# An encoder block on one core: its input projection by seven block products in planned order, and one branch's output product moved into the attention

## The chip, the core and the metric

The kernel runs on one core of a Trainium2 chip. The core has a matrix engine (TensorE, PE in the profile; PEld is its weight load), a vector engine (VectorE, DVE), a scalar engine (ScalarE, ACT), GpSimd (POOL) and SyncE (SP), which here does nothing but issue DMAs. Each engine works through its own queue in order and waits on semaphores. Sixteen DMA engines move data between the device memory (DRAM) and the on-chip memory of 128 partitions; matmuls write into PSUM, a small memory of eight banks of 128 x 512 float32.

The metric is the device time of one execution in microseconds (us). Less is better.

## What is computed

The input x has 2048 tokens of width 1024, in float32. `proj = rms_norm(x) @ w_in` has 4608 columns, which are split into u and v (512 each), q, k and v of an attention (512 each), and two gates of 1024 each.

```python
z_a = gelu(proj[..., :1024])
y_a = gmlp_spatial_gating(z_a[..., :512], z_a[..., 512:], ...)   # layer norm of v, mixing in chunks of 128 tokens, times u
y_b = neighbourhood_attention_2d(q, k, v, ...)                   # q, k normed per head; 8 heads, windows of 8 x 16 on a 32 x 64 grid
gates = sigmoid(gate_pre + b_gate)
merged = gates[..., :1024] * (y_a @ w_o_a) + gates[..., 1024:] * (y_b @ w_o_b)
x = x + merged @ w_out
x = x + square(relu(rms_norm(x) @ w_ff1)) @ w_ff2                # inner width 4096
```

## The kernel before, in words

**Products.** A float32 operand is split into a high part (a cast on ScalarE to fp32r) and a low part (the remainder, on VectorE), and a product is made of three matmuls: high by high, high by low, low by high. One matmul takes a 128 x 128 tile of weights and 512 columns. A product of 128 x 512 with an inner width of 1024 is thus 24 matmuls (`gemm`, L335).

**Order of the work.** The first part, up to the end of the attention, is written as a list: `run` (L1345) calls for each half h of 1024 tokens `gmlp` (L522: u, then v with its layer norm and the spatial mixing `mix`, L577), `att_v` (L640), `qk` (L595) for q and for k, then `gate_units` (L652). Weights are loaded (`load_wk`, L327) and split just ahead; x times the norm's gain is split once for each half (`parts`, L452) and kept on chip in 16 tiles `hT`. The framework's own scheduling sets the order on the engines. `later` and `flush` (L343, L347) put transposes and mixing some products after the work that they wait for. Results go to DRAM: `ya` (first branch, split), `qs`, `ks`, `vs`, and `gt` (gates, 256 KB a tile). `bias_tables` (L396) makes the attention's bias tables by DMAs of GpSimd.

**The attention** (`attention`, L802) has 16 units (4 pairs of heads by 4 row blocks) of 4 steps each. A step i does the scores of step i (`att_scores`: matmuls, a minimum and bias on VectorE, exp on ScalarE, the normalising on VectorE), the transposes of step i-1 (`att_turn`) and the values of step i-2 (`att_values`). Keys come through GpSimd's queue, the rest (`qn`, `vw`, `bias`) through SP's, one unit ahead. Between the steps, `fill` takes the gate tiles of the second half, 24 matmuls each: of 32, up to the 28th is spread over the 64 steps, and 4 follow after.

**The second part** has another discipline: `Plan` (L81). Steps are the pieces of PE work in a fixed order, with a cost in us; chains are stages (loads, casts, remainders, sums) with a cost, an engine and a lead before the step that needs them. `Plan.run` gives each stage the latest step by which it must be issued, issues earlier what fits an engine's modelled clock and the 51 buffers (`NBUF`) of 4 KB per partition, and so writes the engines' order out. `rest` (L1320) puts into one plan, for each half: `merge` (L1001: both branch products, 12 matmuls each, times their gates, added and split), `out_proj` (L1067), `up` (L1198) and `down` (L1280).

**Seven block products.** `up` and `down` cut each operand into 2 x 2 blocks and form seven products of sums of blocks instead of eight (`seven`, L957). The sums of weights are made by four GpSimd operations for each 256 columns (`w_seven`, L893; L909 to L916), those of activations likewise, stored in DRAM as seven parts (`hf`, `af`) and loaded and split again by `x_seven` (L925), in 28 buffers for one operand. One unit of seven products of 4 blocks is 84 matmuls.

Of the kernel before, what the change touches and what calls it, by code (L numbers as in the profile page):

```python
# [12 lines left out]
F32 = mybir.dt.float32  # L13
# [60 lines left out]


# [5 lines left out]
class Plan:  # L81
# [24 lines left out]
    def run(self):  # L106
# [5 lines left out]
        release = [[] for _ in range(n)]  # L112
        for c in self.chains:
            due = at[c.first] if c.first is not None else at[min(n, c.start + 1)] + c.due
            low = (c.start + 1) if c.start is not None else 0
            c.low = min(low, n - 1)
            c.latest = []
            for st in c.stages:
                i = n - 1
                while i > c.low and at[i] > due - st.lead + 1e-9:  # L120
                    i -= 1
                c.latest.append(max(i, c.low))
            for k in range(len(c.latest) - 2, -1, -1):
                c.latest[k] = min(c.latest[k], c.latest[k + 1])
        for _ in range(3):
            for c in self.chains:
                for a, k in c.after:
                    for j in range(k):
                        a.latest[j] = min(a.latest[j], c.latest[0])
# [17 lines left out]
        active, nxt = [], 0  # L147

        def issue(c, i, t):
            k = c.done  # L150
            st = c.stages[k]
            b = max(c.ready, clock.get(st.eng, 0.0), t)
            clock[st.eng] = b + st.cost
            c.ready = b + st.cost + st.wait
# [17 lines left out]
        for i, s in enumerate(self.steps):  # L172
# [5 lines left out]
            for c in active:  # L178
# [3 lines left out]
                if k > c.done:  # L182
                    force(c, k, i, t0)
                    if c.first is not None and c.first <= i:
                        now = max(now, c.ready)
# [5 lines left out]
            for c in active:  # L191
                if c.low > i:
                    continue
                while c.done < len(c.stages):
# [5 lines left out]
                    b = max(r, clock.get(st.eng, 0.0), now)  # L200
# [4 lines left out]
                    c.ready = r  # L205
# [22 lines left out]
class Block:  # L228


    def __init__(self, ctx, tc, a):
        self.ctx, self.tc, self.nc, self.a = ctx, tc, tc.nc, a
        self.waiting = []
        self.second, self.free = False, []
# [16 lines left out]

        self.x1 = d("x1", [2, 8, P, 1024])
# [4 lines left out]
    def first_part(self):  # L257
# [6 lines left out]
        self.part = part  # L264

    def second_part(self):

        self.part.close()
        self.second = True
        self.more = self.ctx.enter_context(self.tc.tile_pool(name="more", bufs=1, reuse_waits="tile"))  # L270
        self.free = list(range(NBUF))

# [5 lines left out]
    def give(self, *ts):  # L278
        self.free += [t for t in ts if t is not None]

    def new(self, shape, dt, name, tag="act"):

        return self.take(shape, dt, name) if self.second else (None, self.slot(shape, dt, name, tag))
# [37 lines left out]
    def split_w(self, raws, name, pool=False):  # L321

        per = raws[0].shape[1]
# [1095 lines left out]
```

## Time and profile before

| | |
|---|---|
| median of 3 runs | 2731.29 us (2729.28 to 2735.18) |
| profiled execution, its own time | 2733.02 us |
| its span, first to last instruction | 2730.6 us |
| mean granted clock of PE in it | 0.982 of full |
| busy: PE, VectorE, ScalarE, GpSimd | 2620.1, 1667.3, 975.4, 869.0 us |
| moved by DMA | 474.11 MB |

The span of the trace runs: input projection to about 666 us, attention to about 1008, the last gate tiles to about 1031, merge and output product to about 1438, then the feed-forward part. Busy time of PE is modelled, since matmuls are pipelined; the distance between the starts of two matmuls tells what one costs. In the rows, `fg<-hT,wg_hi` means that tile fg is written from hT and wg_hi; "x1024" counts instructions; the number after the comma is the mean duration in ns; behind the bar stands the idle time before them and what ended it. In tables of windows, the numbers after the window and its length are busy us of PE, PEld, DVE, ACT and POOL with instruction counts in brackets, then the granted clock of PE, the DMA engines' busy share and GB/s.

### The profile page before, as it was taken

The page shows a single profiled execution, that of the slowest core. Times are in us where ns is not written, and L with a number is a line of the kernel's source. Part 1 is how long each engine was busy: PE and PEld are TensorE (multiplying, and loading weights), DVE is VectorE, ACT ScalarE, POOL GpSimd, SP SyncE. Part 2 cuts the span into 40 slices and gives each one's busy share as a digit, 9 for nine tenths or more (in the row PEclk, how much of TensorE's full clock was granted, in tenths as well). Part 3 has the DMA queues.
Part 4 walks back from the last instruction along what each step waited for, and adds up shares of the span by engine and source line. Part 5 has one row for each costly group of instructions (what it writes and reads, how often), then busy time and mean ns, then how long its engine had stood idle before and what let it go on. Part 6 is the DMA issues. An engine that isn't in the chain of part 4 may idle for free. (4 is left out here: it accounts for less than half of the span.)

```text
span 2730.6 us, 33775 instructions
## 1 busy us (share of the span) xinstructions
PE 2620.1 (96%) x12228; PEld 2133.0 (78%) x12228; DVE 1667.3 (61%) x2574; ACT 975.4 (36%) x1567; POOL 869.0 (32%) x640
## 2 busy tenths in 40 slices
PE   8999999999999997998998999899998999979999
PEld 7888888887777775886876888678886888868887
DVE  6545225546766652543547666788877566588886
ACT  6333225322433321234243434434334343443331
POOL 0005500002121200020035767633433676734341
PEclk9999999999999998999999999999999999989999
DMA  6358842456888838268283444644445544464442
GB/s 193 112 132 199 235 141 89 118 126 150 241 246 231 233 111 308 78 229 326 77 302 129 134 163 148 256 164 158 149 138 195 170 137 160 164 252 141 165 141 104
DMA packets 324630, 474.11 MB, mean 174 GB/s; under 512 B 29485, under 2 KB 215252, under 8 KB 324464
## 3 DMA queue, kind: packets, MB, share of 16 engines
q1 hardware_dynamic: 310176, 444.13, 50.7%
q0 software_dynamic: 13248, 27.82, 4.0%
q8 instruction: 97, 1.59, 0.2%
q14 instruction: 69, 0.57, 0.1%
q10 hardware_dynamic: 1040, 0.00, 0.0%
HBM read 310.78 MB, written 161.04 MB: 173 GB/s over the span
## 5 line engine op out<-in xcount | busy, mean ns | idle before, releaser
L977 PE MATMUL z<-x_t,t_hi 128*128 128x512 f32 x1024 | 321.8, 396 | 39.9 <-DVE x L1304 30.7
L340 PE MATMUL fg<-hT,wg_hi 128*128 128x512 f32 x1024 | 331.4, 398 | 0.0
L870 DVE TENSOR_TENSOR r_lo<-w_r,r_hi 128x1024 fp32r<-128x1024 f32 (+3 forms) x140 | 212.3, 1516 | 81.6 <-ACT r_hi L866 81.6
L977 PEld LDWEIGHTS z<-x_t,t_hi 128*128 128x128 f32 x1024 | 194.4, 191 | 85.7 <-ACT a_B L1226 13.9
L340 PEld LDWEIGHTS fg<-hT,wg_hi 128*128 128x128 f32 x1024 | 191.4, 189 | 44.5 <-issue 8.4
L909 POOL TENSOR_TENSOR w_s<-w_r 128x512 f32<-128x512 f32 (+3 forms) x70 | 98.9, 1412 | 361.1 <-PE y L977 265.8
L977 PE MATMUL z<-x_t,t_lo 128*128 128x512 f32 x512 | 202.2, 395 | 5.7 <-DVE t_lo L870 5.7
L340 PE MATMUL fg<-hT,wg_lo 128*128 128x512 f32 x512 | 202.2, 395 | 0.0
L977 PE MATMUL x<-x_r,t_hl 128*128 128x512 f32 x768 | 192.0, 398 | 6.8 <-DVE t_hl L870 6.8
L977 PEld LDWEIGHTS x<-x_r,t_hl 128*128 128x128 f32 x768 | 147.8, 193 | 39.5 <-DVE t_hl L870 7.6
L866 ACT CAST r_hi<-w_r 128x1024 fp32r<-128x1024 f32 (+3 forms) x140 | 135.9, 972 | 76.3 <-PE z L977 50.2
L340 PE MATMUL fg<-mg,w_out_hi 128*128 128x512 f32 x512 | 160.5, 394 | 2.1 <-DVE mg L1059 2.1
L977 PE MATMUL z<-x_t,r_hi 128*128 128x512 f32 x512 | 159.1, 392 | 2.7 <-DVE x L1304 2.6
L1304 DVE TENSOR_TENSOR x<-z,x 128x512 f32<-128x512 f32 x152 | 104.2, 686 | 90.3 <-PE z L977 90.2
L977 PE MATMUL z<-x_r,r_hi 128*128 128x512 f32 x512 | 159.3, 393 | 0.0
L977 PE MATMUL y<-x_r,r_hi 128*128 128x512 f32 x512 | 158.5, 391 | 0.0
L977 PE MATMUL x<-x_r,r_hi 128*128 128x512 f32 x512 | 157.6, 389 | 0.0
L665 DVE TENSOR_TENSOR g<-fg,rs_row 128x512 f32<-128x512 f32 x64 | 44.1, 691 | 172.1 <-PE fg L340 171.5
L1130 POOL TENSOR_TENSOR h_t<-h,h 128x512 f32<-128x512 f32 x8 | 10.6, 1321 | 390.4 <-ACT h L1119 390.4
L949 DVE TENSOR_TENSOR x_r<-x_r,x_r 128x1024 fp32r<-128x1024 f32 x80 | 131.8, 1660 | 1.5 <-ACT x_r L945 1.5
L870 DVE TENSOR_TENSOR t_lo<-w_s,t_hi 128x1024 fp32r<-128x1024 f32 (+3 forms) x70 | 126.6, 1808 | 3.0 <-ACT t_hi L866 3.0
L687 POOL DMA_DIRECT2D kst<-ks x32 | 24.1, 753 | 322.6 <-DVE y L584 186.2
(219 smaller groups left out, 6060.5 us busy)
## 6 DMA issues: line engine op xcount, KB each, us to landing
w_r<-in_w_ff_dram SPq DMA_DIRECT2D x116, 512.0 KB, 4.4
x_r<-af SPq DMA_DIRECT2D x64, 512.0 KB, 4.5
x<-in_xT_dram SPq DMA_DIRECT2D x32, 512.0 KB, 9.5
wg<-in_w_in_dram SPq DMA_DIRECT2D x32, 512.0 KB, 7.6
gt<-g SPq DMA_DIRECT2D x64, 256.0 KB, 3.0
qn<-qs SPq DMA_DIRECT2D x64, 256.0 KB, 4.9
g<-gt SPq DMA_DIRECT2D x32, 512.0 KB, 12.4
x<-x SPq DMA_DIRECT2D x32, 512.0 KB, 9.0
```

The lines of the kernel that those rows point to most:

```text
L340: self.nc.tensor.matmul(out, w[p], x[q], start=(i == 0 and j == 0), stop=(i == n - 1 and j == 2))
L665: nc.vector.tensor_tensor(g, pt, rs[b][1], ALU.mult)
L687: nc.gpsimd.dma_start(k.rearrange("p r c -> p (r c)"), self.ks[:, :, hd, pair, r0 * GW : (r0 + n) * GW].rearrange("l d t -> (l d) t"),)
L866: nc.scalar.copy(e[name + "_"][1][0], e[name][1])
L870: nc.vector.tensor_tensor(lo, e[name][1], hi.bitcast(F32), ALU.subtract)
L909: nc.gpsimd.tensor_tensor(s23[:, :, 1], r1[:, :, 0], r1[:, :, 1], ALU.subtract)
L949: nc.vector.tensor_tensor(lo, lo.bitcast(F32), hi.bitcast(F32), ALU.subtract)
L977: nc.tensor.matmul(out, a[u], b[v], start=(p in (1, 5, 2) and k == 0 and j == 0), stop=(k == n - 1 and j == 2), skip_group_check=p in (6, ...
L1130: nc.gpsimd.tensor_tensor(t[0][1][:, 1], v[:, 1], u[:, 1], ALU.subtract)
L1304: nc.vector.tensor_tensor(v, bank, v, ALU.add)
```

## The change

- The first part becomes a plan of its own (`first_steps`), with the same 51 buffers. `first_u` makes u of the first half by direct products in quarter steps from x in pieces of 256 KB, and forms the sums of blocks of x on GpSimd. Gates of both halves and u of the second half are units of seven products (`feat`). v with the attention's v (`values`), and q with k (`queries`), are seven products with tokens as rows (`seven_tok`): one slice has 4 x 128 columns of each of the seven parts of x, and the block sums of the weights stay on chip for 8 slices (28 buffers).
- The operands of these go through DRAM: sums of x in `xf`, sums of weights in `wf`, u in `ut`. `x_slice` loads a slice in four DMAs with runs of 512 bytes.
- Gates get their sigmoid before they are stored, in both halves.
- `bias_tables` becomes a chain of GpSimd stages in the plan.
- The attention stays a list. Its filler is no longer gate tiles: `branch_units` makes the 32 tiles of the first branch's output product (12 matmuls each), times the gate, into `ma`. 26 of them are spread (2 ahead), 6 follow.
- `merge` has the second branch's product only; `ma` is added on GpSimd.
- The planner orders what follows what by chains (`hf_done`, `af_done`) instead of given steps, and its costs for loads and GpSimd are lower.

The diff, cut to its core:

```diff
+        self.ut = d("ut", [AW, S])
+        self.ma = d("ma", [D, S])
+        self.xf = d("xf", [2, P, 7, 4, 512])
+        self.wf = d("wf", [2, P, 7, 4, 512])
...
-    DMA, CAST, SUB, ADD = 3.0, 1.06, 1.25, 0.7
-    PSUM_DVE, PSUM_ACT, POOL, MM = 0.7, 0.6, 1.9, 0.2267
+    DMA = 1.6
+    POOL, MM = 1.5, 0.2267
...
+    def feat(self, h, xs, c0, row, act, dst, leads=(26, 15, 10)):
+        w = self.w_seven(self.a["w_in"][0], [0, 2, 4, 6], [1, 3, 5, 7], c0, leads)
...
+        ids = self.seven(w, xs, {1: copy(0, 0, True), 5: copy(1, 1, True), 6: copy(0, 1, False), 3: add(0, 1), 7: add(1, 1),
+                                 2: add(0, 0), 4: (lambda bank: fin(1, 0, bank), 0, {"DVE": 0.7, "ACT": 0.7}, 0)})
...
+    def x_slice(self, h, t):
...
+                src = self.xf[h][:, p0:p1, :, t * P : (t + 1) * P] if n == 2 else self.xf[h][:, p0, :, t * P : (t + 1) * P]
+                nc.sync.dma_start(lo.bitcast(F32), src)
...
+    def seven_tok(self, ws, x, evac, mid):
...
+                for k in range(4):
+                    a = [v[:, k] if xi is None else v[:, xi, k] for v in x[0][xn][1]]
+                    b = [v if wi is None else v[:, wi] for v in ws[k][0][wn][1]]
+                    for j, (u, v) in enumerate(((0, 0), (0, 1), (1, 0))):
+                        nc.tensor.matmul(out, a[u], b[v], start=(p in (1, 5, 2) and k == 0 and j == 0),
+                                         stop=(k == 3 and j == 2), skip_group_check=p in (6, 3, 7, 4))
...
+    def first_steps(self):
+        plan = self.plan = Plan(NBUF)
+        xs = self.first_u()
...
+        for c in range(8):
+            if c < 2:
+                self.first_w(0, c, len(plan.steps) + 5)
+            elif c < 6:
+                self.rows_out(1, c - 2, len(plan.steps) + 5, norm)
...
+            gates(0, xs, c)
...
+        xs = [self.x_seven(self.xf[1][:, :, c], (self.xf_done[1, c],)) for c in range(4)]
...
+            self.feat(1, xs, C_U + c * 256, lambda b: self.rows["in", 1, b], act,
...
+            gates(1, xs, c)
+        for p, f in ((0, self.values), (1, self.queries)):
+            ws = [self.x_seven(self.wf[p][:, :, c], (self.wf_done[p, c],)) for c in range(4)]
+            for h in range(2):
+                for t in range(4):
+                    f(h, t, ws)
...
+        self.bias_tables(mark, end)
+        plan.run()
...
+    def branch_units(self):
+        ys = []
+        for b in range(4):
+            ys.append([])
+            for k in range(4):
+                y = self.slot([2, 512], F32R, "y")
+                nc.sync.dma_start(y.bitcast(F32), self.ya[:, :, k, b * 512 : b * 512 + 512])
+                ys[b].append(y)
+        load = lambda c: self.load_wk(a["w_o_a"][0], c * 256, 256, 4, "woa", True) if c < 4 else None
...
+            g, at = gs.pop(0)
+            pt = self.feat_gemm(w, mm, ys[b], 4)
+            nc.vector.tensor_tensor(g, pt, g, ALU.mult)
+            nc.sync.dma_start(self.ma[at], g)
+            yield
...
-            for name, src in (("ya", self.ya), ("yb", self.yb)):
...
+                        for i, (src, j) in enumerate(((self.ma, m), (self.gt, m + 8))):
+                            nc.sync.dma_start(e["g"][1][:, i], src[j * P : (j + 1) * P, tok : tok + 512])
...
+                    def add(e=e):
+                        g = e["g"][1]
+                        nc.gpsimd.tensor_tensor(g[:, 0], g[:, 0], g[:, 1], ALU.add)
...
+        with self.plan_part("one"), self.tc.manual_schedule():
+            self.first_steps()
+        with self.list_part():
+            self.units, self.bias = {}, {}
+            self.load_unit(0)
+            units = self.branch_units()
+            next(units)
+            next(units)
+            done = 2
...
+                while done < 26 and done < 2 + (step + 1) * 24 / 64:
+                    next(units)
+                    done += 1
...
+        with self.plan_part("two"), self.tc.manual_schedule():
             self.rest()
```

In `first_u`, x comes in pieces of 128 x 512 and each product of u is four steps of six matmuls:

```diff
+                    nc.sync.dma_start(e[raw][1][:, b], a["xT"][k * P : (k + 1) * P, b * 512 : b * 512 + 512])
...
+                for q in range(4):
+                    ks = range(2 * q, 2 * q + 2)
+                    need = [w[g // 2][q // 2][1]] + [A[b, k] for k in ks]
+                    i = plan.step(6 * self.MM, lambda ks=ks: prod(ks), need)
```

In `queries`, each of the four results of a slice (q and k of two token tiles) goes through these stages before its transposes:

```diff
+                ch = plan.chain([Stage("ACT", 0.65, square, 1, 0, 8, 0.3), Stage("DVE", 0.9, factor, 0, 1, 6, 0.6), Stage("DVE", 1.4, scale, 0, 0, 3, 0.2)], start=i)
+                self.todo.append((delay, lambda: turn(ch)))
```

## Rows read from the trace of the kernel before

**Rows 1.** The page, busy us of PE, share of the span, instructions.

```profile
PE 2620.1 (96%) x12228; PEld 2133.0 (78%) x12228; DVE 1667.3 (61%) x2574; ACT 975.4 (36%) x1567; POOL 869.0 (32%) x640
```

**Rows 2.** The chain that ended last: start us, us, what; a feed-forward piece.

```profile
1478.98 2.72 PE z L977 x12
```

**Rows 3.** Windows of 100 us: the first, and one within `up`.

```profile
0.00:100.00 100.00, 91.58 (x421) 74.86 (x422) 61.16 (x106) 50.38 (x80) 0.70 (x6) 1.00 0.49 153
...
1500.00:1600.00 100.00, 100.00 (x443) 82.84 (x442) 61.21 (x60) 40.39 (x58) 66.75 (x41) 1.00 0.44 150
```

**Rows 4.** Groups of instructions by line, PE, high part: gates, one projection, u.

```profile
L340 PE MATMUL fg<-hT,wg_hi 128*128 128x512 f32 x1024 | 331.4, 398 | 0.0
...
L340 PE MATMUL tg<-wk_hi,hT 128*128 128x512 f32 x256 | 82.9, 395 | 0.0
...
L340 PE MATMUL fg<-hT,wu_hi 128*128 128x512 f32 x256 | 82.0, 399 | 8.3 <-ACT hT L455 7.8 <-DVE z L534 0.3
```

**Rows 5.** Groups by line, POOL: one of four sums of blocks in `out_proj`.

```profile
L1131 POOL TENSOR_TENSOR h<-h 128x512 f32<-128x512 f32 x8 | 11.2, 1398 | 0.6
```

**Rows 6.** Windows of 100 us: three changes of operands in the feed-forward part.

```profile
1700.00:1800.00 100.00, 87.20 (x367) 69.98 (x367) 74.13 (x77) 42.33 (x60) 55.94 (x40) 0.95 0.67 242
2000.00:2100.00 100.00, 89.05 (x378) 72.17 (x376) 76.86 (x85) 37.72 (x49) 32.12 (x24) 0.97 0.57 195
2400.00:2500.00 100.00, 86.08 (x350) 68.80 (x351) 81.67 (x87) 40.78 (x51) 37.38 (x21) 0.91 0.55 193
```

**Rows 7.** The chain that ended last, at the first of these.

```profile
1751.38 9.05 DMA x_r<-af
1762.11 7.84 DMA af<-a_A
```

**Rows 8.** Timeline of PE at the end of the queries: start, us, what, idle before.

```profile
665.68 1.08 PE L623 MATMUL qT<-ident,qn 128*128 128x128 f32 x4 [5.95 <-DVE qn L611]
...
673.67 0.60 PE L623 MATMUL qT<-ident,qn 128*128 128x128 f32 x4
674.03 0.71 PE L340 MATMUL fg<-hT,wg_hi 128*128 128x512 f32 x2
```

**Rows 9.** Groups by line, DVE: operations of queries and keys, and one remainder of weights.

```profile
L605 DVE TENSOR_REDUCE qms<-sq 128x8 f32<-128x512 f32 x32 | 21.9, 684 | 62.6 <-ACT sq L603 62.6
L611 DVE TENSOR_TENSOR qn<-tg,qrs 128x512 f32<-128x512 f32 x32 | 22.1, 691 | 1.9 <-DVE qrs L609 1.0
L626 DVE SCALAR_TENSOR_TENSOR qo<-qT,qg,qo 128x512 fp32r<-128x512 f32 x16 | 11.9, 744 | 1.5 <-ACT qo L625 1.5
L364 DVE TENSOR_SCALAR rsq_t<-rsq_t 128x8 f32<-128x8 f32 (+1 forms) x44 | 10.7, 242 | 1.4
L609 DVE TENSOR_SCALAR qrs<-qrs,rs_col 128x8 f32<-128x8 f32 x32 | 10.2, 318 | 1.1
L308 DVE TENSOR_TENSOR wq_lo<-wq,wq_hi 128x1024 fp32r<-128x1024 f32 x8 | 9.8, 1226 | 55.7 <-ACT wq_hi L307 54.9
```

**Rows 10.** Groups by line, POOL: DMAs that write the bias tables.

```profile
L424 POOL DMA_DIRECT2D tb<-tbi x72 | 43.0, 600 | 31.5 <-DMA tb<-tbi 26.7 <-DMA tb<-tbt 3.5 <-issue 0.9
```

**Rows 11.** The attention as one window: all instructions; those of the gates (L340) alone.

```profile
666.00:1008.00 342.00, 336.42 (x2178) 259.38 (x2178) 223.43 (x750) 127.81 (x395) 66.04 (x55) 0.99 0.79 218
...
666.00:1008.00 342.00, 183.55 (x672) 122.80 (x672) 0.99 0.79 218
```

**Rows 12.** DMA issues between 680 and 1000 us: count, KB each, us to landing.

```profile
wg<-in_w_in_dram SPq DMA_DIRECT2D x12, 512.0 KB, 7.6
```

**Rows 13.** Windows of 10 us: early attention, start of the merge, end of `out_proj`.

```profile
690.00:700.00 10.00, 10.00 (x69) 7.14 (x69) 7.83 (x30) 3.85 (x14) 1.06 (x2) 1.00 1.06 257
1040.00:1050.00 10.00, 5.80 (x12) 3.63 (x12) 1.23 (x1) 1.04 (x1) 0.00 (x0) 0.55 1.02 364
1400.00:1410.00 10.00, 10.00 (x45) 8.26 (x44) 3.72 (x5) 2.31 (x3) 9.25 (x7) 1.00 1.03 416
```

**Rows 14.** Timeline of PE at the start of the merge.

```profile
1043.28 1.22 PE L340 MATMUL fg<-y,w_o_a_hi 128*128 128x512 f32 x2 [12.58 <-ACT w_o_a_hi L866]
```

More of the change, by code (lines that the diff above doesn't have):

```diff
@@ L73, in __init__, with begin @@
         self.ends = []
+    def begin(self):
+        k = self.done
+        return 0.0 if k and self.stages[k].eng == self.stages[k - 1].eng else self.ready
 class Step:
@@ L147, in run @@
         active, nxt = [], 0
+        needs = [[] for _ in range(n)]
+        for c in self.chains:
+            if c.first is not None and c.last is not None:
+                needs[c.first].append(c)
         def issue(c, i, t):
@@ L183, in run @@
                     force(c, k, i, t0)
-                    if c.first is not None and c.first <= i:
-                        now = max(now, c.ready)
+            now = max([now] + [c.ready for c in needs[i]])
             late = now - t0
@@ L278, in give @@
     def give(self, *ts):
-        self.free += [t for t in ts if t is not None]
-    def new(self, shape, dt, name, tag="act"):
-        return self.take(shape, dt, name) if self.second else (None, self.slot(shape, dt, name, tag))
+        self.free += ts
     def slot(self, shape, dt=F32, name="slot", tag="act"):
@@ new lines, in stores, with out, f @@
+    def stores(self, e, names, dst, give):
+        def out(name, part, kept):
+            def f():
+                p0, p1 = self.X_PART[part]
+                self.nc.sync.dma_start(dst[:, p0:p1] if p1 - p0 == 2 else dst[:, p0], e[name][1])
+                if kept:
+                    self.give(e[name][0])
+            return f
+        return [Stage("SP", self.DMA if p != "t4" else 0.5 * self.DMA, out(n, p, g), 0, int(g), 3 - 0.5 * i, 2.0)
+                for i, (n, p, g) in enumerate(zip(names, ("r1", "r2", "t23", "t4"), give))]
@@ new lines, in first_w, with load @@
+    def first_w(self, pair, c, due):
+        cols = ((C_V, C_AV), (C_Q, C_K))[pair]
+        e = {}
+        st = []
+        for i, raw in ((0, "w1"), (1, "w2")):
+            def load(e=e, raw=raw, k=2 * c + i):
+                e[raw] = self.take([2, 512], F32, raw)
+                for j in range(2):
+                    self.nc.sync.dma_start(e[raw][1][:, j], self.a["w_in"][0][k * P : (k + 1) * P, cols[j] : cols[j] + 512])
+            st.append(Stage("SP", 3.0, load, 1, 0, 26, 3.0))
+        st += self.sums(e, "w1", "w2", "t23", "t4", "S")
+        st += self.stores(e, ("w1", "w2", "t23", "t4"), self.wf[pair][:, :, c], (True,) * 4)
+        ch = self.plan.chain(st)
+        ch.first = due
+        self.wf_done[pair, c] = (ch, len(st))
@@ L1185, in turn_evac @@
             nc.scalar.copy(row, own["pt"])
-            self.rows[h, b] = row
+            self.rows[key, h, b] = row
+            self.cols[key, h, b] = own["col"]
             if b == 1:
```

1061 lines of the change are left out of this document (651 added, 410 removed).

## The prediction

> **What bounds the kernel now.** I read the busy table first: TensorE (PE) is busy in 96% of the span [rows 1]. A busy PE need not be PE at its peak, so the chain that ended last came next: in a stage without waits it consists of pieces of twelve matmuls that take 2.72 us, 0.2267 us for each [rows 2]. The table of 100 us stretches shows PE without a gap in such a stage, and a gap of 8.4 us in the first stretch [rows 3]. So the kernel is bound by the number of its matmuls, plus some 110 us of gaps. Where a change takes matmuls out, the question is what new gaps it opens, and whether another engine or the DMA is next in line.
>
> **Matmuls removed.** The groups of PE by line give the counts [rows 4]: gates 1024 with the high part of the weights (the low part has half as many, as everywhere), so 1536; the four projections of which wk is one, 384 each; wu 384. That is 3456 matmuls. In the new kernel the first half's u stays direct (192). All else goes through seven block products instead of eight: 3264 x 7/8 = 2856. So 408 matmuls go, 408 x 0.2267 = **-92.5 us**, all of it on PE, which sets the end. The two branch products keep their number (768); half of them move into the attention. Work in transposes, spatial mixing and norms stays.
>
> **The start.** x arrives in 256 KB pieces and u goes in quarter steps. The gap was 8.4 us [rows 3]; the first product still waits for one weight tile, one piece of x and their casts. Between -2 and +10; I take **+2**.
>
> **Block sums of x.** They can start only when a block's scaled casts and squares are done, and the gates need all of them. They are 16 GpSimd operations like the one of 1398 ns [rows 5], 22 us, plus one weight's four sums, beside 192 x 0.2267 = 43.5 us of u products. Nothing, if the sums end in time; 15 us, if they begin when half of the u products are through. I take **+6**, nearer to nothing because u covers most.
>
> **Changes of operands.** A set of 28 buffers is exchanged three times that the kernel before does not have: gates of the first half to u of the second, gates to values, values to queries. The nearest rows are the three exchanges of the feed-forward part, whose stretches lack 12.8, 11.0 and 13.9 us of PE [rows 6]. Part of that was a load that waited for a store just made, 9.1 us of loading behind 7.8 us of storing on the chain [rows 7]. Here xf and wf were stored long before, so that part goes; but 16 casts' remainders come onto VectorE (DVE) at once. Bounds 9 (three times 3, the casts alone) to 38 (three times 12.6); I take **+24**, 8 each.
>
> **Values and queries.** One slice of the new loop does 84 matmuls, 19.0 us. A slice of queries adds four groups of four transposes, 0.36 us each by two starts [rows 8], so PE needs 20.5 us. DVE per slice [rows 9]: three remainders of 1024 columns at 1.23 and one of 512 at 0.69 (4.4); three sums of a bank at 0.69 (2.1); four norms of 0.68 + 0.32 + 0.69 and six short operations of about 0.2 (2.9 each, 11.6); four low parts at 0.745 (3.0). That is 21.1 us, 21.9 with the gaps between short operations. So DVE, not PE, bounds the queries: 8 x 1.4 = 11 at least. Bounds 0 (gaps filled from the neighbouring slice) and 30; I take **+13**. Values have 3 remainders of 1024 columns, 16 operations of 512 and some short ones, 16.5 us, under PE's 20.5; but ScalarE's sqrt stands in the middle of their chain: 0 to 10, I take **+2**. SP issues some 24 DMAs per slice of values, about 12 of 20 us; nothing.
>
> **Bias tables.** Their steps, some 130, now stand on GpSimd's queue among the weight sums, from the second half's u on. The largest group has 72 DMAs of 0.60 us and stood 26.7 us in waits for other DMAs [rows 10]; whoever waits for a sum behind such a wait is a cast of weights, then a product. The sums of a gate unit take 6 of 19 us, those of xf or wf 6 more, so 7 us per unit are left to cover it. 0 to 10 us; I take **0**.
>
> **The attention, and the step before it.** In the window from the last transposes to the last value product, 342 us, PE is busy 336.4 us, and 672 matmuls of it are gates: 152.3 us. So the attention itself takes 184.1 us of PE, 2.9 in each of 64 steps [rows 11]. With 24 units of 12 matmuls in place of 28 gate tiles of 24, PE needs 184.1 + 65.3 = 249.4, with the 5.6 us of gaps as now 255. This is already in the -92.5; the question is what holds the stage up above 255. DVE has 223.4 us of work there [rows 11], minus 28 and plus 24 gate products: 221, below PE. The DMA engines are 0.79 busy at 218 GB/s [rows 11]: 74.6 MB, or 276 GB/s while busy. What changes: 28 gate stores go (7.3 MB), and the weights for gates, of which 12 loads of 512 KB stand in most of the window [rows 12] (6.3); in come gate loads and product stores of 24 units (12.6), three w_o_a tiles (1.6), and 16 tiles of ya (8.4), which the list of work places ahead of everything, behind the last query stores on SP's queue. Together 83.6 MB: at 276 GB/s 303 us, at the 257 GB/s of a full window of small packets [rows 13] 325 us. The low end is 255. Here the cover goes: half as much filler hides a late key or query tile. The step before already waits 5.95 us for the last normed queries [rows 8], then gates ran; now the first branch products need ya, w_o_a and GpSimd's split first. I take 290 us for the stage with its start, **+35**: nearer to the DMA's end because the same bytes must go in less time, but not at it, since ya is needed only bit by bit and the last steps load nothing.
>
> **Merge.** The start of the merge waited 12.6 us [rows 14], with the DMA at full share, 364 GB/s, and the granted clock at 0.55 right after [rows 13]. The last store of the stage before still comes ahead of the first load on SP's queue, so the wait stays; then half as many y tiles and weights are needed. But products come twice as fast for each gate tile. Sigmoid leaves ScalarE here, one sum moves from DVE to GpSimd (1.4 us, beside 2.72 of products). -15 to +10, I take **-6**. The planner's new costs and dependences move feed-forward loads too; with no row for that, -10 to +10, zero.
>
> **Sum.** -92.5 + 2 + 6 + 24 + 13 + 2 + 35 - 6 = -16.5. The profiled execution took 2733.0 us, so 2716.5; the median of the runs is 1.7 below it: 2715.
>
> **Rivals.** *One: PE sets the attention after all.* For it: PE is 98% busy there now while the DMA already moves 218 GB/s, and some windows move 416 GB/s at full share [rows 13]. Then the stage takes 255 instead of 290, and with the exchanges at their low end (9 instead of 24) the time is 2715 - 35 - 15 = 2665. Against it: that window moves large packets. The Trainium skill, page DMA: Bandwidth & Descriptors, section Specifications, says that transfers of 512 bytes and more reach line rate and that a core's share of HBM is about 358 GB/s; an estimate by that page is 83.6 MB / 358 = 233 us, under PE's 255, so by the page this rival would hold. The rows disagree with both halves of it, 257 GB/s at a full share and 416 elsewhere.
>
> *Two, slower: the attention at the rate of its own small packets.* Place: the loads of keys, queries, values and biases behind 8.4 MB of ya. Price: 325 us instead of 290, so 2750. It decides from 306 us on (290 + 16.5), that is below 273 GB/s; the full windows show 257 [rows 13], the mean while busy 276 [rows 11]. Against it: the packets' time is partly queueing, and PE had slack for it.
>
> *Three: DVE and the exchanges take more than half of it back.* Queries at their 30 and exchanges at 38: +17 and +14, so 2746. For it: DVE is at 21.9 of 20.5 us when the last exchange falls on it. Against it: the feed-forward part runs DVE at 0.77 to 0.82 in such stretches [rows 6].
>
> *Four: the matmuls go, other gaps replace them, and nothing can be told from no change*: the sum is only 16.5 us away from that. It lies inside the forecast's own range and takes 0.07 of its chance.
>
> **How the numbers follow.** Forecast 0.42 (own range 2690 to 2740), rival one 0.27, rival two 0.20, rival three 0.11. A measurement of this kernel can tell about 0.2% from no change, 5.5 us. Of the forecast's 0.42, 0.27 lies faster, 0.07 within (rival four), 0.08 slower. Rival one is faster; rivals two and three are slower but for 0.02 within and 0.02 faster, where other terms come out low. Together: faster 0.56, same 0.09, slower 0.35. The range takes in rivals one and two and the upper bounds of exchanges and queries: 2655 to 2775.
>
> **What would show it.** In the new trace: about 9960 matmuls of 512 columns (408 fewer); steady gate stretches with PE full; in the queries DVE over 0.95 busy, PE lower; three dips of PE by 5 to 10 us at the exchanges; the stage from the last transposes to the last value product near 290 us with the DMA over 0.9. PE over 98% there means rival one; waits of scores or transposes on keys, queries or values mean rival two. The prediction is wrong in its working if the first 800 us hold gaps over 90 us or under 30, or if the feed-forward part moves by over 10.

## The result, and the profile after

The changed kernel takes 2808.1 us (median of 4 runs, 2806.7 to 2810.1), 1.028 times the kernel before, 95% interval 1.0263 to 1.0298. The forecast was 2715 with a range of 2655 to 2775: wrong in sign, and above the range.

The page's busy line and its DMA line, to be read beside [rows 1]:

```profile
PE 2561.2 (91%) x11820; PEld 2071.9 (74%) x11820; DVE 1857.1 (66%) x2781; ACT 1159.6 (41%) x1802; POOL 1105.1 (39%) x800
DMA packets 419164, 573.76 MB, mean 205 GB/s; under 512 B 33901, under 2 KB 283156, under 8 KB 418992
```

The 408 matmuls are gone, but PE's busy time fell by 59 us only, and its idle time rose from 110 to 244 us. The DMA moves 100 MB more. The windows by stage (us, then busy us of PE, PEld, DVE, ACT, POOL with counts, granted clock, DMA share, GB/s): u of the first half; gates and the second u; values; queries; the gap; the attention with its last branch products; merge to the end.

```profile
0.00:86.47 86.47, 53.98 (x216) 42.33 (x217) 48.93 (x62) 48.89 (x68) 34.03 (x30) 0.88 0.39 122
86.47:460.00 373.53, 358.05 (x1541) 291.85 (x1541) 243.39 (x247) 191.32 (x256) 199.67 (x129) 0.97 0.73 250
460.00:686.00 226.00, 179.37 (x794) 147.18 (x795) 134.63 (x219) 106.93 (x142) 78.25 (x130) 0.90 0.92 245
686.00:880.20 194.20, 174.71 (x807) 138.67 (x805) 168.09 (x404) 96.18 (x167) 0.00 (x0) 0.98 0.69 178
880.20:927.70 47.50, 0.02 (x2) 0.00 (x1) 1.43 (x2) 1.97 (x2) 2.18 (x3) 0.50 1.03 322
927.70:1231.40 303.70, 285.01 (x1888) 211.44 (x1888) 210.44 (x743) 124.64 (x392) 38.01 (x37) 0.94 0.93 256
1244.60:2804.90 1560.30, 1510.05 (x6576) 1240.45 (x6576) 1049.50 (x1106) 588.62 (x776) 752.91 (x472) 0.98 0.53 181
```

Length minus PE's busy time is the idle time of a stage: 32.5, 15.5, 46.6, 19.5, 47.5 and 18.7 us up to the attention's end. Where PE waits most, the DMA share is over 0.9 (values, gap), except at the start. The last row is the good part: from the merge to the end it took 1687.3 us before (1043.28 [rows 14] to 2730.6), now 1560.3. That is 127 less, of which 384 matmuls (87 us) were moved out. The merge still starts after a gap of 13.2 us, as in [rows 14].

PE's timeline shows the gaps: two at the start, four of those in the values, then the one of 47 us, which stands where [rows 8] had 5.95.

```profile
41.88 1.87 PE L1631 MATMUL ms<-ones,acc 128*128 128x1 f32 x8 [6.77 <-DVE acc L464]
86.47 1.22 PE L1452 MATMUL z<-r,r_hi 128*128 128x512 f32 x2 [13.75 <-DVE z L544]
474.55 4.88 PE L682 MATMUL z<-x_t,x_t 128*128 128x512 f32 x12 [7.55 <-ACT vg L714]
526.45 4.56 PE L682 MATMUL z<-x_t,x_t 128*128 128x512 f32 x12 [9.68 <-ACT vg L714]
560.65 4.53 PE L682 MATMUL z<-x_t,x_t 128*128 128x512 f32 x12 [6.93 <-ACT vg L714]
586.67 5.12 PE L682 MATMUL z<-x_r,x_t 128*128 128x512 f32 x12 [11.53 <-DVE av L726]
927.70 1.22 PE L350 MATMUL fg<-y,woa_hi 128*128 128x512 f32 x2 [47.48 <-POOL woa_hi L320]
```

The releasers in the values (a copy of a bank, a sum) are not the cause: ScalarE, which makes the copies and scales what the sums add, waits for DMAs itself.

```profile
518.33 0.62 ACT L654 CAST x_t<-x_t 128x512 fp32r<-128x512 f32 x1 [2.20 <-DMA x_t<-xf]
524.87 1.04 ACT L654 CAST x_r<-x_r 128x1024 fp32r<-128x1024 f32 x1 [3.81 <-DMA ya<-ya]
...
560.01 0.59 ACT L714 COPY vg<-z 128x512 f32<-128x512 f32 x1 [7.70 <-DMA ya<-ya]
...
579.77 0.62 ACT L793 CAST ya<-y 128x512 fp32r<-128x512 f32 x1 [13.97 <-DMA vs<-av]
```

The first of these waits for a load of the next slice's operands. The others name stores of results (`ya`, `vs`) that they do not read; each of these three instructions takes a new buffer in the kernel's text, so what they wait for is most likely a buffer that the store has to leave. So the next view is SP's queue, here beside the bias tables' transfers (start, us of SP, line, tile):

```profile
513.41 6.54 SPq L801 DMA_DIRECT2D ya<-ya  x2
520.07 16.17 SPq L814 DMA_DIRECT2D vs<-av  x16
...
543.29 7.30 SPq L801 DMA_DIRECT2D ya<-ya  x2
550.68 26.58 SPq L814 DMA_DIRECT2D vs<-av  x16
577.31 0.39 SPq L646 DMA_DIRECT2D x_t<-xf  x1
```

Each of those 16 stores takes SP 1.0 to 1.7 us, the next operand loads (L646) stand behind them, and the buffers that they read come free only after them. SP's queue also shows the gap of 47 us: 15.9 us of SP for the branch operands, ahead of the first weight.

```profile
897.03 1.40 SPq L1118 DMA_DIRECT2D bias<-tb  x3
898.48 15.89 SPq L1284 DMA_DIRECT2D y<-ya  x16
915.20 0.85 SPq L333 DMA_DIRECT2D woa<-in_w_o_a_dram  x1
```

These readings name suspects. Which of them costs time, the runs had to tell. A difference between two kernels that were measured in different batches is that of their ratios to the kernel before, times 2732 us.

### The profile page after: what moved, and what is told of

Its sections match the earlier page's. It is cut to its first block, busy times and chain, and to the rows that moved or that the text cites. A ratio compares the mean times of both kernels' runs of the same rounds, so it can differ in the third digit from the quotient of the medians.

```text
span 2804.9 us, 34089 instructions
## 1 busy us (share of the span) xinstructions
PE 2561.2 (91%) x11820; PEld 2071.9 (74%) x11820; DVE 1857.1 (66%) x2781; ACT 1159.6 (41%) x1802; POOL 1105.1 (39%) x800
## 3 DMA queue, kind: packets, MB, share of 16 engines
q8 instruction: 93, 1.52, 0.2%
## 5 line engine op out<-in xcount | busy, mean ns | idle before, releaser
L1452 PE MATMUL z<-x_t,t_hi 128*128 128x512 f32 x1184 | 372.7, 396 | 39.4 <-DVE x L1768 28.2
L1345 DVE TENSOR_TENSOR r_lo<-w_r,r_hi 128x1024 fp32r<-128x1024 f32 (+3 forms) x176 | 286.3, 1628 | 82.0 <-ACT r_hi L1341 58.1
L1384 POOL TENSOR_TENSOR w_s<-w_r 128x512 f32<-128x512 f32 (+3 forms) x88 | 117.8, 1339 | 456.7 <-PE y L1452 261.2
L1452 PE MATMUL z<-x_t,t_lo 128*128 128x512 f32 x592 | 234.2, 396 | 1.5 <-DVE t_lo L1345 1.5
L1341 ACT CAST r_hi<-w_r 128x1024 fp32r<-128x1024 f32 (+3 forms) x176 | 173.7, 988 | 85.2 <-PE z L1452 62.7
L1128 POOL DMA_DIRECT2D kst<-ks x32 | 26.5, 831 | 446.8 <-DMA ks<-qo 263.7
L1420 ACT CAST x_r<-x_r 128x1024 fp32r<-128x1024 f32 x104 | 107.6, 1050 | 143.8 <-DVE t_hl L1345 99.9
L1391 POOL TENSOR_TENSOR w_s<-w_r,w_s 128x512 f32<-128x512 f32 (+3 forms) x88 | 151.3, 1719 | 37.0 <-DVE t_lo L1345 10.0
L1390 POOL TENSOR_TENSOR w_s<-w_r 128x512 f32<-128x512 f32 (+3 forms) x88 | 159.5, 1812 | 4.8
L350 PE MATMUL fg<-mg,w_hi 128*128 128x512 f32 x512 | 158.0, 389 | 0.9 <-DVE mg L1525 0.9
L1385 POOL TENSOR_TENSOR w_r<-w_r,w_r 128x512 f32<-128x512 f32 (+3 forms) x88 | 148.7, 1690 | 7.6 <-DMA w_r<-in_w_in_dram 0.6
L1420 ACT CAST x_t<-x_t 128x1024 fp32r<-128x1024 f32 (+1 forms) x104 | 84.6, 835 | 122.3 <-PE x L1452 80.6
```

Source lines behind the costliest of these rows:

```text
L350: self.nc.tensor.matmul(out, w[p], x[q], start=(i == 0 and j == 0), stop=(i == n - 1 and j == 2))
L1128: nc.gpsimd.dma_start(k.rearrange("p r c -> p (r c)"), self.ks[:, :, hd, pair, r0 * GW : (r0 + n) * GW].rearrange("l d t -> (l d) t"),)
L1341: nc.scalar.copy(e[name + "_"][1][0], e[name][1])
L1345: nc.vector.tensor_tensor(lo, e[name][1], hi.bitcast(F32), ALU.subtract)
L1384: nc.gpsimd.tensor_tensor(s23[:, :, 1], r1[:, :, 0], r1[:, :, 1], ALU.subtract)
L1385: nc.gpsimd.tensor_tensor(r1[:, :, 1], r1[:, :, 1], r2[:, :, 1], ALU.add)
```

## The experiments

**The change cut into three.** First the planner alone, in the kernel before:

```diff
-    DMA, CAST, SUB, ADD = 3.0, 1.06, 1.25, 0.7
-    PSUM_DVE, PSUM_ACT, POOL, MM = 0.7, 0.6, 1.9, 0.2267
+    DMA = 1.6
+    POOL, MM = 1.5, 0.2267
...
-                    win[k] = self.x_seven(self.af[h, k], self.af_at[h, k] + (7 if k >= NU - 2 else 0))
+                    win[k] = self.x_seven(self.af[h, k], (self.af_done[h, k],))
```

> The kernel before with nothing but the change's planner in its second part (new search, chains that wait for the stores they read, SP cost 1.6, POOL cost 1.5); the first part, the attention with the gates and the merge with two products are as before. Theory A, the 40 us that the second part gained beyond its 384 matmuls come from the merge, which moves less per us: the time is within 5 us of 2731. Rival B, they come from the planner: 2700 to 2720. Rival C, the planner's shorter costs let operands come late: 2736 or more.

2712.1 us, ratio 0.9926 (0.9911 to 0.9940): rival B, 20 us faster than before, and the fastest kernel of this study. The windows up to 1043 us are as before; the gain lies behind:

```profile
1043.30:2710.60 1667.30, 1606.63 (x6960) 1316.83 (x6960) 1087.46 (x1178) 620.18 (x818) 699.56 (x440) 0.98 0.53 177
```

That is 20 us less than 1687.3 for the same 6960 matmuls. With the planner's old costs put back:

```diff
-    DMA = 1.6
-    POOL, MM = 1.5, 0.2267
+    DMA = 3.0
+    POOL, MM = 1.9, 0.2267
```

> The kernel before with the change's planner but the old costs (3.0 us for an SP transfer, 1.9 us for a GpSimd sum). The planner with the new costs gave 2712 against 2732. Theory A, the gain is in the new costs, which let SP's and GpSimd's stages be placed nearer to what they take: this stays within 5 us of 2732. Theory B, the gain is in the search and in the chains that wait for the stores they read, in place of a step written by hand: 2705 to 2718.

2717.9 us, ratio 0.9944 (0.9928 to 0.9961). Theory B: by the medians three quarters of the gain come from the search and from chains that wait for the stores which they read. That the new costs give the rest is not shown, since the two intervals overlap.

Next, the branch product's move without the new input projection:

```diff
-        with self.plan_part("one"), self.tc.manual_schedule():
-            self.first_steps()
...
+            self.gmlp(h, raws, xs, hT, rs)
+            self.att_v(h, hT, rs)
...
+            gates = self.gate_units(h, hT, rs)
...
+            for _ in gates:
+                pass
+        self.flush()
         units = self.branch_units()
```

> The second part of the change alone: the input projection is that of the kernel before (24 matmuls a product, operands in SBUF), the second half's gates run before the attention, and the attention, the merge and the planner are the change's. Matmuls as before the change in number. Theory A, the input projection from DRAM is where most of the change's loss lies, and the attention with the branch product still ends by its bytes: 666 us to the values and keys' end, + 28 gate units of 24 x 0.2267 = 152, + 305 for the attention (83 MB at 272 GB/s), + 13 for the merge's start, + 1560 for the rest as in the changed kernel = about 2700, 2680 to 2720. Rival B, without the boundary's operand loads the attention is PE-bound (264 us): 2650 to 2675. Rival C, the branch product in the attention is itself the loss: 2735 or more.

2725.7 us, ratio 0.9973 (0.9962 to 0.9984), between theories A and C. Its projection up to 841.6 us and its attention:

```profile
0.00:841.60 841.60, 825.89 (x3764) 682.86 (x3765) 350.66 (x683) 254.93 (x388) 142.29 (x176) 1.00 0.52 147
841.60:1147.10 305.50, 284.72 (x1889) 210.99 (x1887) 213.42 (x744) 127.93 (x394) 28.66 (x32) 0.94 0.91 255
1160.60:2721.60 1561.00, 1513.36 (x6576) 1241.79 (x6576) 1049.45 (x1106) 588.34 (x776) 753.55 (x472) 0.98 0.54 181
```

Attention and rest last as long as in the changed kernel (303.7 and 1560.3). Without the change's projection PE is idle for 16 us up to the attention; with it the attention starts 86 us later. So the three parts, added in this order, are: planner -20 us, branch product moved +13 (0.9973 - 0.9926), input projection **+84** (1.028 - 0.9973). The last includes the gap of 47 us ahead of the attention: in the list-built kernel gates stand between queries and attention, and SP issues the 16 operand loads of the branch product under them, from 677 to 840 us.

**The gap and the attention.** The branch operands put later, so that only the first block's four loads stand ahead of the attention:

```diff
-        for b in range(4):
-            ys.append([])
...
+        y_load(0)
+        yield
...
+            if u in (0, 2, 4):
+                y_load(u // 2 + 1)
...
-            next(units)
-            done = 2
+            done = 0
```

> Of the branch product's 16 operand loads only the first block's four are issued before the attention, the other three blocks one pair of products ahead of their use; the two products ahead of the first scores move behind the third step's values. Theory A, the order on SP's queue makes the 47.5 us gap (the 16 loads take 15.9 us of SP ahead of the first weight load, whose cast then waits): the first scores of the attention start when their operands land, near 902, the gap falls to 18 to 25 us, and the time falls by 18 to 30 us, to 2778 to 2790. Rival B, from 880 us to the attention's end the bytes set the time (89.85 MB at 272 GB/s = 330 us): the gap shrinks but the attention grows by as much, and the time is within 6 us of 2808.

2808.6 us, ratio 1.0274 (1.0259 to 1.0290): no change, rival B, and the trace shows it plainly. The gap fell to 26.5 us, and later products waited for the same loads; the merge began at 1243.4 instead of 1244.6.

```profile
906.58 1.19 PE L350 MATMUL fg<-y,woa_hi 128*128 128x512 f32 x2 [26.52 <-DMA y<-ya]
...
928.79 1.22 PE L350 MATMUL fg<-y,woa_hi 128*128 128x512 f32 x2 [6.74 <-DMA y<-ya]
```

So not the order but the transfers. More of them, then fewer:

```diff
             nc.sync.dma_start(g, self.gt[at])
+            nc.sync.dma_start(g, self.gt[at])
```

> Each of the 32 gate loads of the branch product is issued twice (8.4 MB more in the attention, nothing else). Theory A, from the end of the queries to the end of the attention the bytes set the time: 8.4 MB at the 272 GB/s measured there are 31 us, so 2830 to 2845. Rival B, the attention is held by the order of work on TensorE, VectorE and ScalarE: within 8 us of 2808.

2833.5 us, ratio 1.0374 (1.0355 to 1.0393): +26 us for 8.4 MB. The gap stays at 47.4 us, the attention behind it grows from 303.7 to 327.5. In the other direction, the operands of the first token block serve all four blocks (the kernel leaves out what the other three would read):

```diff
-            ys.append([])
-            for k in range(4):
+            ys.append([] if b == 0 else ys[0])
+            for k in range(4 if b == 0 else 0):
```

> The branch product uses the operands of its first token block for all four blocks: 12 of the 16 operand loads (6.3 MB) ahead of the attention are left out, nothing else is moved. Theory A (after the run in which the loads were only put later, and the time stayed), from the queries' end to the attention's end the transfers set the time: 6.3 MB at 272 GB/s are 23 us, so 2780 to 2792, with a gap at the attention's start near 30 us and an attention no longer than before. Rival B, the attention loses by the order of its engines and only the gap's place changes: within 8 us of 2808.

2793.4 us, ratio 1.0219 (1.0195 to 1.0243): -17 us for 6.3 MB, all of it in the gap, which is 31.1 us; the attention behind it is no shorter (308.8 us). Both follow theory A, at 2.6 to 3.1 us for each MB. At the stage's mean (91.31 MB from 880 to 1222 us at 267 GB/s) it would be 3.7, so most of what bytes would cost at that rate shows in the time, not all of it.

**Values and bias tables.** First the tables moved to the queries:

```diff
             ws = [self.x_seven(self.wf[p][:, :, c], (self.wf_done[p, c],)) for c in range(4)]
+            mark = len(plan.steps)
...
-        c = self.plan.chain([Stage("POOL", 1.0, f, t, gv, 5 + 2.2 * (n - i), 0.0) for i, (f, t, gv) in enumerate(fs)], start=start)
+        c = self.plan.chain([Stage("POOL", 1.0, f, t, gv, 5 + 1.0 * (n - i), 0.0) for i, (f, t, gv) in enumerate(fs)], start=start)
```

> The bias tables' GpSimd work is held back until the queries begin (it ran between about 500 and 620 us, under the values). Theory A, the tables' small transfers slow SP's own issues (a store took 1 to 2.5 us of SP's time there against 0.3 to 0.5 elsewhere) and so the values' operands: TensorE's gaps between 475 and 616 us (7.6 + 9.7 + 2.9 + 6.9 + 11.5 + 5.7 = 44 us) shrink to under 10 us, the queries, which move less (174 GB/s), take some of it back, and the time falls by 15 to 40 us, to 2768 to 2793. Rival B, the values are held by the DMA engines anyway (share 1.04 at 269 GB/s in 460 to 500 us, before the tables): the gaps stay, and the time is within 8 us of 2808. Rival C, the slow issues go with the tables into the queries: values without gaps, queries longer by as much, time within 8 us.

2817.0 us, ratio 1.0303 (1.0286 to 1.0321). Neither gain nor cover: the values' waits on operands are gone, and the queries have them instead (rival C; the 6 us more are not clear of noise, the two intervals overlap). The two stretches of the values, then one of the queries:

```profile
500.00:560.00 60.00, 60.00 (x285) 50.08 (x284) 44.36 (x80) 36.28 (x49) 0.00 (x0) 1.00 0.83 220
560.00:620.00 60.00, 58.05 (x280) 48.61 (x279) 42.83 (x74) 32.05 (x44) 0.00 (x0) 1.00 0.79 215
...
750.00:800.00 50.00, 34.67 (x139) 26.49 (x140) 24.98 (x61) 16.26 (x28) 20.59 (x34) 0.84 0.91 214
```

Then eight of the nine tables left out; every bias load reads as many bytes from the one that is left:

```diff
-                add(f)
+                if (ct, kind) == (1, 1):
+                    add(f)
...
-        src = self.tb[ct][kind][2 * pair : 2 * pair + 2].rearrange("h r c k -> (r c) h k")
+        src = self.tb[1][1][2 * pair : 2 * pair + 2, :, :, :w].rearrange("h r c k -> (r c) h k")
```

> Of the 93 stores that fill the bias tables only the 8 of one table are made (2.0 of 12.4 MB), and every bias load reads as many bytes from that one table: the other eight tables are left out. Theory A, the tables cost the values about their bytes at the rate of that stage (10.4 MB at 242 GB/s = 43 us): the gaps of 475 to 616 us fall to under 10 and the time to 2755 to 2778. Rival B, the GpSimd queue's transfers were beside the point and x's operand loads hold the values alone: within 8 us of 2808.

2779.0 us, ratio 1.0175 (1.0157 to 1.0194): -29 us. The values keep the 7.0 us at their first products and 1.6 later, and the queries end 29.5 us earlier. That is less than the 43 of theory A; why was not tested. The 16 stores of a slice take SP 7 to 9 us, with one exception, beside loads of the queries' weights and before the one table's stores begin (691 us):

```profile
651.27 16.17 SPq L814 DMA_DIRECT2D vs<-av  x16
```

The DMA share was 0.90 from 650 to 670 us there. So slow issues need no table stores beside them. Is it SP's queue, or the DMA engines behind it? Two runs. First the operands of x, stored by slices of tokens so that they load in runs of 2 KB:

```diff
-        self.xf = d("xf", [2, P, 7, 4, 512])
+        self.xf = d("xf", [2, P, 7, 4, 4, P])
```

> The stored block sums of x are laid out by slices of 128 tokens, so that the values' and queries' operand loads move runs of 2 KB where they moved runs of 512 B; the stores and the second half's gate operands move runs of 512 B in turn, in a stage where the DMA engines are 0.64 to 0.85 busy. The bytes are the same. Theory A, in the values and queries the DMA engines' time is what ends last, and a packet has a cost of its own there (40.6 ns for a mean of 697 B in 460 to 690 us, 80 ns for 1737 B in 240 to 460 us): the values' and first queries' gaps shrink, and the time falls by 10 to 25 us, to 2783 to 2798. Rival B, the bytes alone count, or SP's and GpSimd's issue of transfers: within 6 us of 2808. Rival C, the 512 B runs now hurt the gates instead: 2815 or more.

2807.5 us, ratio 1.0273 (1.0254 to 1.0293): nothing. From 460 to 690 us SP's queue of transfers made 39245 packets instead of 61414 for about as many bytes (43.44 and 42.84 MB), and took 62.9% of the engines' time instead of 67.7%. PE's gaps in the values are as large as before (45 us against 44). The length of the runs is not it. Then half of the slow stores issued by ScalarE (`q` is its queue for b = 1):

```diff
-                            nc.sync.dma_start(vs[row + r], e["av"][1][r * GW + k0 : r * GW + k0 + n, b])
+                            q.dma_start(vs[row + r], e["av"][1][r * GW + k0 : r * GW + k0 + n, b])
```

> In the values, the eight stores of the attention's v for the second token tile are issued by ScalarE instead of SP; the tables, the loads and the bytes stay. (With the tables beside them, 16 of these stores took 16 to 27 us of SP's time, without the tables 7 to 8, and the next slice's operand loads stand behind them.) Theory A, SP's queue is what holds the operands: with half of these stores gone, SP needs some 8 to 13 us less per slice for the three or four slices beside the tables, the gaps of 44 us fall below 25, and the time falls by 10 to 25 us. Rival B, the DMA engines themselves are the limit (share 0.83 to 0.92 there), SP's slow issues only show it: within 6 us of 2808. Rival C, the issues now block ScalarE, whose copies of the products' results wait: 2815 or more.

2836.5 us, ratio 1.0376 (1.0359 to 1.0393): rival C, 26 us slower. On ScalarE the issues are as slow as on SP, and the copy behind them frees no bank:

```profile
519.91 17.86 ACTq L814 DMA_DIRECT2D vs<-av  x8
537.80 0.58 ACT L714 COPY av<-x 128x512 f32<-128x512 f32 x1 [17.37 <-DMA vs<-av]
```

Meanwhile SP needed up to 9.4 us for a single operand load, against 0.4 to 2.5 in the changed kernel. So a second queue issues no faster, which speaks for a limit behind the queues. What in the tables' transfers makes it (their count, their stores, GpSimd's part in them) was not separated.

**The start.** The casts of the first block sums held behind the last row copy (L1653), which had stood behind them on ScalarE's queue, as the trace of the changed kernel shows:

```profile
82.34 1.04 ACT L1341 CAST t_hi<-t 128x1024 fp32r<-128x1024 f32 x1 [3.19 <-POOL t L428]
83.56 1.05 ACT L1341 CAST t_hi<-t 128x1024 fp32r<-128x1024 f32 x1 [0.17 <-POOL t L425]
84.52 0.58 ACT L1653 COPY rs_row<-rs_T 128x512 f32<-128x512 f32 x1
```

```diff
-                 "t23": plan.chain(self.hilo(e, "t23", [2, 512], 3), af, hold=self.kept(e, "t23", 2)),
+                 "t23": plan.chain(self.hilo(e, "t23", [2, 512], 3), af, start=turned, hold=self.kept(e, "t23", 2)),
```

> The casts of the first half's block sums are held until the last row copy of the first u products (they stood ahead of it on ScalarE's queue, waiting for GpSimd). Theory A, the 13.75 us gap at 86.5 us is that order on ScalarE: the row copy at 84.5 goes to about 73, the gap falls to 3 to 7 us, the first gate product comes 6 to 10 us earlier, and the time falls by 5 to 10 us. Rival B, the sums on GpSimd (from 62.5 to 85 us) set it, and the gap only moves to the product that reads the first sum: less than 3 us.

2801.5 us, ratio 1.0248 (1.0226 to 1.0269): theory A. The gap of 13.75 us became one of 2.00, at 75.38 us; part of it came back as nine waits of 0.5 to 2.7 us for sums and remainders. Net -9 us by the ratios, whose intervals just overlap (1.0263 to 1.0269); in the profiled execution the attention starts 6.7 us earlier.

The first weight sums kept off GpSimd during the first norm:

```diff
+                if b == 0:
+                    nc.gpsimd.tensor_copy(self.sm(4, "held"), self.cols["in", 0, 0])
...
+            raw = self.plan.chain([Stage("POOL", 0.0, lambda: None, 0, 0, leads[1])] * 2 + sums, ((got, 2),), start=self.quiet)
```

> GpSimd's sums of the first gate weights and of the first value weights (10.4 us of work at 26 to 37 us) are held until the first rows of the norm are turned, behind 51 us. Theory A, VectorE is slowed while GpSimd works (sums of squares of 128x512 took 1.77 us there and 0.68 us elsewhere), and that is the 6.77 us gap ahead of the first norm's columns: the gap falls to 1 to 3 us and the first gate product comes 3 to 6 us earlier. Rival B, the squares wait for the raw x and for ScalarE, and the gap stays at 5 to 7 us. Rival C, the held sums are late for the first gate product: slower by 5 us or more.

2809.4 us, ratio 1.0277 (1.0260 to 1.0294). Four of the six sums were held (two still ran, at 29.5 to 32.5 us). The gap of 6.77 fell to 3.71 and the norm's columns came 2.9 us earlier, but the first gate product came at 88.06 instead of 86.47 us: it waits for the late row copy, and that gap grew to 19.67 us. Theory A in its place, nothing in the time.

**Three together.** Edits of three runs above (eight tables and 12 operand loads left out, casts held):

> Three of the edits at once: eight of the nine bias tables left out, 12 of the 16 branch operand loads left out (the first block's operands serve all four), and the first block sums' casts behind the row copy. Alone they gave about 29, 15 and 7 us. Theory A, the losses add up: 2808 - 51 = 2757, within 8 us, and what is left above the list-built projection's 2726 (some 30 us and the 92 us of matmuls that were saved) is in the start, the changes of operands, the queries' end, the rest of the gap before the attention and the lower clock. Rival B, one wait hides another (the operand loads left out only let the attention's own transfers end earlier, where the tables had already given room): 2770 or more. Rival C, without them the projection is TensorE-bound: 2735 or less.

2755.1 us, ratio 1.0070 (1.0047 to 1.0094): theory A, the losses add up (57 us against 29 + 17 + 9). Without these losses the kernel is still 26 us slower (1.0070 - 0.9973) than with the list-built projection.

## Why the prediction was wrong

**Right.** The count: 12228 - 11820 = 408 matmuls. The changes of operands, +24: at the second u 5.6 us (3.92 + 1.65), at the values 9.1 (1.52 + 7.55), at the queries some 7. The values' own work, +2, where the tables do not run: PE is busy 22.00 of the 22 us from 648 to 670. The merge's start stays. Queries, +13: a steady slice takes 22.0 us, 1.5 more than the 20.5 of PE in the working, 12 for eight slices. So the size was right, but the reason was not:

```profile
770.86 0.63 PE L893 MATMUL qT<-ident,k 128*128 128x128 f32 x4 [0.66 <-DVE k L876]
...
792.89 0.63 PE L893 MATMUL qT<-ident,k 128*128 128x128 f32 x4 [0.66 <-DVE k L876]
```

Of the 1.5 us, 0.7 is this wait; the rest is PE's own, 21.4 us busy in a slice. In a steady stretch PE is the fuller engine and VectorE is at 0.86, not over 0.95:

```profile
780.00:800.00 20.00, 19.34 (x93) 15.49 (x92) 17.17 (x41) 10.20 (x19) 0.00 (x0) 1.00 0.76 197
```

**Bias tables, 0: the step that failed in its reasoning.** It looked at GpSimd's queue and the weight sums behind it, found 7 us per unit of cover, and did not ask what the tables' transfers do to other transfers. Before, they ran at 232 to 344 us, beside gates with operands on chip, and PE was busy 249.2 of the 250 us from 250 to 500. Now they ran beside a stage that loads its operands and stores its results for every slice. Leaving eight of nine out gave 29 us, and the move to the queries showed that no cover was there either.

**Attention with its start, +35: mis-sized by 52.** The mechanism was rival two's, the transfers. From the last transposes to the last value product it took 342.1 us, not 290 (nor rival two's 325):

```profile
880.20:1222.30 342.10, 275.96 (x1851) 204.27 (x1850) 209.36 (x741) 126.24 (x393) 40.19 (x40) 0.87 0.96 267
```

The kernel before took 342 us too [rows 11], so halving the filler bought the stage nothing. The working had 83.6 MB; 91.3 were moved. 32 gate loads and 28 product stores fell into the stage, where the working had 24 of each (3.1 MB), and a fourth w_o_a load (0.5); the first unit's loads come in too (SP issues them from 888.8 to 898.4 us). The same count holds for PE: 346 matmuls of the branch product ran in it, not 288, and PE was busy 276 us, not 249. And "not at it, since ya is needed only bit by bit" was wrong: the run that loads ya bit by bit gained nothing. Rival two's place was not right either: it put the waits at loads of keys, queries and values, but 47.5 us stood ahead of the first branch product, and the attention behind the gap moved 256 GB/s, its figure of 257. That the attention itself is longer than PE's work does not hang on the projection: 305.5 us in the list-built kernel, 303.7 here, for 271 us by the working's prices (184.1 and 32 units of 2.72). PE is busy 285 of the 303.7, at a granted clock of 0.94; the doubled gate loads show that bytes lengthen this stretch, but PE's own pace has a part in it that was not separated. Rival one fell with this: the estimate from the Trainium skill (DMA: Bandwidth & Descriptors, Specifications) put 83.6 MB at 233 us, a rate of 358 GB/s; the stage moved 267.

**Start and block sums, +8: mis-sized by 17.** PE idles 32.5 us in the first 86.47, against 7.9 in the list-built projection, so +25. The working put the sums beside u, but not what their casts do on ScalarE's queue: 13.75 us stood behind a row copy, and by the ratios 9 of that were recovered.

**The matmuls' price.** -92.5 assumed 0.2267 us for each. Up to 880.2 us PE was busy for 766.1 us; the list-built projection has 825.9, so 733.4 would remain. About 7 of the other 33 are in the queries at a granted clock of 1.00 (21.4 us for a slice, not 20.5). Most of the rest stand beside a granted clock of 0.88 and 0.90 at the start and in the values, where PE stops again and again (1.00 in the list-built projection). A gap may thus have cost more than its length; this was not in the working, and how much of the 33 is the clock was not measured by itself.

**The second part, -6 and 0: mis-sized in the other direction.** The planner gave 20 us (bounds were -10 to +10), the lighter merge about 19 more (1667.3 - 87 - 1561).

In sum: of the 92.5 us of matmuls 33 came back as busy time, and idle time up to the attention's start rose from 16 us (list-built) to 162. That is the +86 at which the attention starts later. The terms that missed, 52 + 29 + 17 + 33 - 20 - 13, make 98, and the forecast was 93 too low; the closeness is partly luck, since the gaps and the matmuls' price overlap. The largest failure, 52 + 29, is that the values, the tables and the attention depend on the same transfers, and the working priced the tables by GpSimd's queue alone and the attention by too few bytes, and below the time that these take. The working's own signs of failure came true: PE idles 106 us in the first 800, over its 90, and the second part moved by 40 beyond the moved matmuls, over its 10. One reading in it was off without consequence: rival three took VectorE at 0.77 to 0.82 from [rows 6], which show 0.74 to 0.82.

## What to carry to other kernels

Where operands leave the chip's memory, count each stage's bytes, its neighbours' included, against the rate while the DMA is full: work that cost nothing beside on-chip operands (the tables) was paid for in both places where it was tried here. A gap in which the DMA is full is tested by taking bytes out, not by reordering alone: the reordered run moved 21 us of gap and no time. And a change in several parts is run in parts: the one that had seemed to be an accessory, the planner, was the only one that gained, 20 us.

## What was not expected of the hardware

In the first norm VectorE is slower while GpSimd works. A sum of squares of 128 x 512 takes 0.68 us, and 1.77 beside GpSimd's sums (26.3 to 36.7 us):

```profile
32.10 1.77 DVE L464 TENSOR_TENSOR acc<-acc,sq 128x512 f32<-128x512 f32 x1
33.80 3.45 DVE L494 SCALAR_TENSOR_TENSOR r<-w,g,r 128x512 fp32r<-128x512 f32 x2
37.17 0.68 DVE L464 TENSOR_TENSOR acc<-acc,sq 128x512 f32<-128x512 f32 x1
```

The Trainium skill, GPSIMD Engine Reference, section Specifications, says that GpSimd's interface to the on-chip memory is shared with VectorE, with contention for VectorE instructions that have two inputs there; these have two, and the trace agrees, at 2.6 times the duration.

Issuing a transfer is not a fixed cost: a store of 48 or 64 KB took 0.45 us of SP's time (7.07 us for 16) without the tables and 1.7 (26.58 for 16) with them, and 2.2 on ScalarE (17.86 for 8). A slice without table stores took 1.0 (16.17 for 16), at a DMA share of 0.90. What sets it was not found.
